# Final RMSNorm of a decoder trunk: sixteen tile buffers instead of six, and the loads in a loop of their own

## The chip, the cores and the metric

One core of a Trainium2 chip runs the whole program in one launch. The metric is the device time in microseconds, the median of several runs; lower is better. The profile is of one further execution.

## The reference, cut to what matters

The network has two residual layers over 2048 tokens of width 1024, each followed by a mixture of experts, and ends with one RMSNorm over every token. Only that last step is touched:

```python
def rmsnorm(x, gain):
    xf = x.astype(jnp.float32)
    y = xf * lax.rsqrt(jnp.mean(xf * xf, axis=-1, keepdims=True) + EPS)
    return (y * gain.astype(jnp.float32)).astype(x.dtype)
...
    return rmsnorm(x, final_norm)
```

So 2048 x 1024 float32 numbers (16 tiles of 128 rows, 512 KB each) are read, every row is scaled by its own factor and by the vector `final_norm`, and the same amount is written.

## The kernel before, in words

The trunk (`trunk`, L1661) runs layer 0, its experts, the DeltaNet mixer, its output projection, the second set of experts and then `final` (L1029). The experts scatter their rows into `acc`, a DRAM tensor, through indirect DMAs of GpSimd (L838), and end in a loop with a run-time count (`tc.For_i`, L985); every engine passes that point before `final` begins, so nothing of `final` runs beside the experts.

`final` opens the pool `fin`, loads the gain vector spread over 128 partitions into `fr` (L1033), and then has one loop over the NT = 16 tiles. Tile t is loaded from `acc` into `xin` (L1036; six buffers of 4 KB in each partition), ScalarE squares it and sums each row into `ss` (L1039), `rstd` turns the sum into a factor with a small VectorE instruction (L187) and a power on GpSimd (L189), VectorE multiplies the tile by the factor and by `fr` in place (L1041), and the tile is stored to the output (L1042). `ss1`, `rs1t` and `rs1` have four buffers each, from the pool `small` (L75).

All loads and stores of `final` are issued by SyncE (SP), on one queue, and SP issues in the order of its instruction list: a store that waits for VectorE holds up every load behind it. The list's order is made when the program is built. A scheduler takes the instructions that are ready in its own timing and, among those, the one written first. In the order that it made here SP has four loads, the four stores of the same tiles, four loads, and so on, although six buffers are there. The scheduler also gives the DMAs of this queue eight completion semaphores in turn, and a DMA waits until the one that had its semaphore before it has landed, so at most eight are in flight.

Of the kernel before, what the change touches and what calls it, by code (L numbers as in the profile page):

```python
# [6 lines left out]
F32 = mybir.dt.float32  # L7
# [9 lines left out]
P = 128  # L17
S = 2048
D = 1024
KD = D // P  # L20
EPS = 1e-6
NT = S // P
# [48 lines left out]
class Trunk:  # L71
# [957 lines left out]
    def final(self, out, l=1):  # L1029
        tc, nc = self.tc, self.nc  # L1030
        with tc.tile_pool(name="fin", bufs=3, reuse_waits="tile") as pool:
            fr = pool.tile([P, D], F32, name="fr", bufs=1)
            nc.sync.dma_start(fr, self.ins["final"].to_broadcast([P, D]))  # L1033
            for t in range(NT):
                x = pool.tile([P, D], F32, name="xin", bufs=6)
                nc.sync.dma_start(x, self.acc[t * P:(t + 1) * P])  # L1036
                ss = self.small.tile([P, 1], F32, name="ss1")
                sq = pool.tile([P, D], BF16, name="sqo", bufs=1)
                nc.scalar.activation(sq, x, AF.Square, accum_out=ss)  # L1039
                r = self.rstd(ss, 1.0 / D, 1, "rs1")  # L1040
                nc.vector.scalar_tensor_tensor(x, x, r, fr, op0=ALU.mult, op1=ALU.mult)  # L1041
                nc.sync.dma_start(out[t * P:(t + 1) * P], x)  # L1042
# [654 lines left out]
```

## Time and profile before

| what | us |
|---|---|
| median of 3 runs (lowest to highest) | 3322.71 (3316.65 to 3327.7) |
| the profiled execution, its own time | 3314.97 |
| span of its instructions | 3313.2 |
| first load of `final` issued | 3249.73 |
| `final` to the end of the span | 63.5 |

The profiled execution lies 7.74 us under the median of the runs, and its span 1.8 us under its own time. The times in the trace count from the start of the span. `final` is the last 1.9% of it. An engine or a DMA queue is read as busy, or as waiting for what ended its idle time. The DMA share is the mean busy share of the core's 16 DMA engines in a stretch; values a little over 1 come from overlapping records.

### The profile page before, as it was taken

What the parts mean: (1) busy time and instruction counts of PE and PEld (TensorE: products, weight loads), DVE (VectorE), ACT (ScalarE), POOL (GpSimd) and SP (SyncE); (2) the same over time, 40 slices, a digit from 0 to 9 for tenths busy, and PEclk for the clock granted to TensorE, in tenths of its full rate; (3) what the DMA queues carried; (4) which work ended last, traced back from release to release, by engine and by line L of the source; (5) the groups of instructions that cost most, each with busy time, mean ns of one, the idle gap of its engine ahead of it and who ended that gap; (6) DMA issues with size and microseconds to landing.
All of it is one profiled execution on the core that took longest, in us unless ns stands there. A gap on an engine that the chain in (4) does not pass through costs nothing. (4 is left out here: it accounts for less than half of the span.)

```text
span 3313.2 us, 41885 instructions
## 1 busy us (share of the span) xinstructions
PE 2908.4 (88%) x14192; PEld 2313.6 (70%) x14192; DVE 2443.9 (74%) x3805; ACT 1495.1 (45%) x2560; POOL 1022.7 (31%) x877
## 2 busy tenths in 40 slices
PE   4979878787999997999989999988988996999991
PEld 3756666566777774888867877777987765777770
DVE  4998999757878875777876786858445556888783
ACT  6135233216656546443444433444772214666552
POOL 0142323333443431322212131235530212434431
PEclk9989999898999998999999999998999997999996
DMA  6225233638999854545352343457957437989876
GB/s 222 85 73 209 83 132 127 216 121 303 309 281 298 268 169 160 171 153 191 136 174 83 104 144 106 144 148 223 268 195 227 153 121 253 308 279 297 264 232 217
DMA packets 384984, 633.37 MB, mean 191 GB/s; under 512 B 111232, under 2 KB 245504, under 8 KB 384768
## 3 DMA queue, kind: packets, MB, share of 16 engines
q1 hardware_dynamic: 355904, 563.38, 49.9%
q0 software_dynamic: 28864, 67.30, 8.7%
q8 instruction: 113, 1.85, 0.2%
q14 instruction: 103, 0.84, 0.1%
HBM read 484.46 MB, written 175.44 MB: 199 GB/s over the span
## 5 line engine op out<-in xcount | busy, mean ns | idle before, releaser
L260 PE MATMUL pm<-hh,wh 128*128 128x512 f32 x1408 | 565.9, 402 | 0.8 <-ACT wh L237 0.7
L262 PE MATMUL pm<-hh,wl 128*128 128x512 f32 x1408 | 556.5, 396 | 3.6 <-DVE wl L238 3.6
L261 PE MATMUL pm<-hl,wh 128*128 128x512 f32 x1408 | 555.4, 395 | 4.2 <-DVE hl L233 4.2
L238 DVE TENSOR_TENSOR wl<-wr,wh 128x1024 fp32r<-128x1024 f32 x384 | 452.2, 1218 | 40.7 <-ACT wh L237 37.3
L237 ACT ACTIVATE wh<-wr 128x1024 fp32r<-128x1024 f32 x384 | 399.5, 1057 | 134.7 <-PE py L851 56.8
L838 POOL DMA_INDIRECT acc<-ys,ixs x102 | 263.5, 2584 | 435.3 <-DVE wl L238 149.6
L261 PEld LDWEIGHTS pm<-hl,wh 128*128 128x128 f32 x1408 | 269.2, 191 | 63.4 <-DVE hl L233 4.6
L260 PEld LDWEIGHTS pm<-hh,wh 128*128 128x128 f32 x1408 | 269.1, 191 | 62.5 <-issue 4.6
L262 PEld LDWEIGHTS pm<-hh,wl 128*128 128x128 f32 x1408 | 268.6, 191 | 62.9 <-DVE wl L238 5.7
L817 PE MATMUL pu<-wh,xt 128*128 128x512 f32 x656 | 268.8, 410 | 0.5 <-ACT xt L237 0.5
L818 PE MATMUL pu<-wl,xt 128*128 128x512 f32 x656 | 261.3, 398 | 0.0
L819 PE MATMUL pu<-wh,xt 128*128 128x512 f32 x656 | 260.3, 397 | 0.0
L238 DVE TENSOR_TENSOR wl<-wraw,wh 128x1024 fp32r<-128x1024 f32 x88 | 110.9, 1261 | 155.4 <-ACT wh L237 155.2
L286 DVE SCALAR_TENSOR_TENSOR acc<-cin,wfir,acc 128x512 f32<-128x512 f32 (+1 forms) x320 | 214.7, 727 | 0.1
L536 PE MATMUL po<-woh,yh 128*128 128x512 f32 x512 | 172.4, 413 | 30.6 <-ACT yh L237 22.1
L237 ACT ACTIVATE wh<-wraw 128x1024 fp32r<-128x1024 f32 x88 | 93.2, 1059 | 227.4 <-PE pm L261 227.2
L1220 DVE SCALAR_TENSOR_TENSOR dacc<-ub,cols,dacc 128x1024 f32<-128x1024 f32 x144 | 186.8, 1297 | 2.8
L536 PE MATMUL po<-wol,yh 128*128 128x512 f32 x512 | 166.6, 405 | 0.0
L536 PE MATMUL po<-woh,yl 128*128 128x512 f32 x512 | 165.5, 402 | 0.3 <-DVE yl L238 0.3
L795 POOL DMA_INDIRECT xg<-hn,ixs x102 | 112.4, 1102 | 162.6 <-PE tp L805 87.3
L189 POOL TENSOR_TENSOR rs<-rs1t,expo 128x1 f32<-128x1 f32 x48 | 28.3, 589 | 381.1 <-DVE rs1t L187 339.6
L819 PEld LDWEIGHTS pu<-wh,xt 128*128 128x128 f32 x656 | 124.1, 189 | 30.8 <-DVE xt L238 0.5
(377 smaller groups left out, 6362.2 us busy)
## 6 DMA issues: line engine op xcount, KB each, us to landing
wr<-in_w_up_dram SPq DMA_DIRECT2D x256, 512.0 KB, 7.6
wr<-in_w_down_dram SPq DMA_DIRECT2D x128, 512.0 KB, 7.0
modw<-in_modwT_dram SPq DMA_DIRECT2D x96, 512.0 KB, 5.1
wraw<-in_w_in_dram SPq DMA_DIRECT2D x88, 512.0 KB, 3.6
stin<-stg SPq DMA_DIRECT2D x32, 1280.0 KB, 10.4
yr<-yT SPq DMA_DIRECT2D x32, 512.0 KB, 4.7
acc<-xo SPq DMA_DIRECT2D x32, 512.0 KB, 4.1
hn<-ho SPq DMA_DIRECT2D x32, 512.0 KB, 3.2
```

The costliest lines, as they stand in the source:

```text
L237: a = nc.scalar.activation(h, x, AF.Copy) if eng == "act" else nc.vector.tensor_copy(h, x)
L238: return a, nc.vector.tensor_sub(l, x, h.bitcast(F32))
L260: nc.tensor.matmul(ps, wh[:, k], hh[:, k], start=k == 0, stop=False)
L261: nc.tensor.matmul(ps, wh[:, k], hl[:, k], start=False, stop=False)
L262: nc.tensor.matmul(ps, wl[:, k], hh[:, k], start=False, stop=k == KD - 1)
L286: self.tap = nc.vector.scalar_tensor_tensor(o, x, w, i, op0=ALU.mult, op1=ALU.add)
L536: nc.tensor.matmul(ps[:, ns], a[:, k], b[:, ns], start=k == 0 and i == 0, stop=k == KD - 1 and i == 2)
L817: nc.tensor.matmul(ps, xh[:, k], uh, start=k == 0, stop=False)
L818: nc.tensor.matmul(ps, xh[:, k], ul, start=False, stop=False)
L819: nc.tensor.matmul(ps, xl[:, k], uh, start=False, stop=k == KD - 1)
L838: st = nc.gpsimd.indirect_dma_start(out=self.acc, out_offset=bass.IndirectOffsetOnAxis(ap=ix[:, 0:1], axis=0), in_=ys, in_offset=None, bou ...
L1220: nc.vector.scalar_tensor_tensor(acc, ub[:, i:i + 1024], self.col("dn_conv", si * 4 + i), acc, op0=ALU.mult, op1=ALU.add)
```

## The change

The loop is cut in two. The first loop allocates all sixteen tiles (`bufs=NT`, 64 KB in each partition instead of 24 KB) and issues all sixteen loads; the second does the arithmetic and the stores, as before. No instruction that computes or moves data is added or removed.

```diff
             fr = pool.tile([P, D], F32, name="fr", bufs=1)
             nc.sync.dma_start(fr, self.ins["final"].to_broadcast([P, D]))
+            xs = []
             for t in range(NT):
-                x = pool.tile([P, D], F32, name="xin", bufs=6)
+                x = pool.tile([P, D], F32, name="xin", bufs=NT)
                 nc.sync.dma_start(x, self.acc[t * P:(t + 1) * P])
+                xs.append(x)
+            for t, x in enumerate(xs):
                 ss = self.small.tile([P, 1], F32, name="ss1")
                 sq = pool.tile([P, D], BF16, name="sqo", bufs=1)
                 nc.scalar.activation(sq, x, AF.Square, accum_out=ss)
```

## Rows read from the trace of the kernel before

**Rows 1.** The chain that ended last, from 3240 us on: shares by line.
```profile
by line: DMA xin<-acc 24.8%; issue 18.7%; POOL rs L189 10.4%; DVE xin L1041 9.7%; DMA acc<-ys,ixs 6.6%; ACT sqo L1039 4.3%; DVE rs1t L187 3.0%; SPq L1036 1.3%; SPq L1042 1.2%; POOLq L1693 0.7%; SPq L985 0.5%; SPq L1033 0.4%; POOLq L944 0.3%
```

**Rows 2.** Timeline of SP's queue (start, us, what; one line merges several).
```profile
3249.73 0.34 SPq L1033 DMA_DIRECT2D fr<-in_final_dram  x1
3250.12 2.15 SPq L1036 DMA_DIRECT2D xin<-acc  x4
3258.86 6.35 SPq L1042 DMA_DIRECT2D out_dram<-xin  x4
3265.26 2.27 SPq L1036 DMA_DIRECT2D xin<-acc  x4
3273.81 6.54 SPq L1042 DMA_DIRECT2D out_dram<-xin  x4
...
3295.10 2.26 SPq L1036 DMA_DIRECT2D xin<-acc  x4
3303.01 6.54 SPq L1042 DMA_DIRECT2D out_dram<-xin  x4
```

**Rows 3.** Waits in `final`: total us, times, longest; ScalarE, then SP's queue.
```profile
ACT sqo L1039 <- DMA xin<-acc: 45.6, 5, 16.2
SPq L1042 <- DVE rs1t L187: 38.5, 12, 6.6
SPq L1042 <- DVE xin L1041: 6.5, 4, 1.7
```

**Rows 4.** Windows: stretch, us, PE, PEld, DVE, ACT, POOL busy, PEclk, DMA share, GB/s.
```profile
3249.73:3313.20 63.47, 0.00 (x0) 0.00 (x0) 21.94 (x32) 18.39 (x32) 8.68 (x16) 0.50 0.72 273
3254.00:3258.00 4.00, 0.00 (x0) 0.00 (x0) 0.60 (x2) 2.30 (x4) 0.57 (x1) 0.50 1.01 405
3260.90:3261.60 0.70, 0.00 (x0) 0.00 (x0) 0.05 (x2) 0.00 (x0) 0.54 (x1) 0.50 0.10 35
3265.30:3268.30 3.00, 0.00 (x0) 0.00 (x0) 0.00 (x0) 0.00 (x0) 0.00 (x0) 0.50 0.87 273
6.00:26.00 20.00, 4.99 (x16) 2.59 (x16) 9.07 (x23) 14.02 (x18) 1.02 (x1) 1.00 1.02 400
3304.00:3305.00 1.00, 0.00 (x0) 0.00 (x0) 1.00 (x2) 0.74 (x2) 0.00 (x0) 0.50 1.04 422
3311.82:3313.20 1.38, 0.00 (x0) 0.00 (x0) 0.00 (x0) 0.00 (x0) 0.00 (x0) 0.50 0.00 0
```

**Rows 5.** Timeline of the engines: first tile, then multiplies of the second group.
```profile
3255.53 1.06 ACT L1039 ACTIVATE sqo<-xin 128x1024 bf16<-128x1024 f32 x1 [16.18 <-DMA xin<-acc]
3257.55 1.29 DVE L1041 SCALAR_TENSOR_TENSOR xin<-xin,rs,fr 128x1024 f32<-128x1024 f32 x1 [0.69 <-POOL rs L189]
...
3276.63 1.28 DVE L1041 SCALAR_TENSOR_TENSOR xin<-xin,rs,fr 128x1024 f32<-128x1024 f32 x1 [0.72 <-POOL rs L189]
...
3278.70 1.29 DVE L1041 SCALAR_TENSOR_TENSOR xin<-xin,rs,fr 128x1024 f32<-128x1024 f32 x1 [0.72 <-POOL rs L189]
```

**Rows 6.** The instructions of `xin` from 3243 us on: ns min/median/max, starts.
```profile
L1036 SPq DMA_DIRECT2D xin<-acc x16: 376/431/783, 3250.1 to 3297.0; - x16
L1039 ACT ACTIVATE sqo<-xin x16: 1056/1056/1057, 3255.5 to 3303.6; 128x1024 bf16<-128x1024 f32 x16
L1041 DVE SCALAR_TENSOR_TENSOR xin<-xin,rs,fr x16: 1284/1285/1286, 3257.6 to 3307.9; 128x1024 f32<-128x1024 f32 x16
L1042 SPq DMA_DIRECT2D out_dram<-xin x16: 332/335/338, 3258.9 to 3309.2; - x16
```

**Rows 7.** Issue to landing of L1036's loads, then of L1042's stores.
```profile
DMA to landing us min/median/max: 4.4/6.0/7.5
...
DMA to landing us min/median/max: 2.6/2.6/3.0
```

**Rows 8.** Small instructions of `final` grouped by line (busy us, mean ns, idle before).
```profile
L189 POOL TENSOR_TENSOR rs<-rs1t,expo 128x1 f32<-128x1 f32 x16 | 8.7, 542 | 54.1 <-DVE rs1t L187 42.2 <-DMA xin<-acc 11.8
L1039 ACT ACTIVATION_READ_ACCUMULATOR sqo<-xin 128x1 f32 x16 | 3.0, 186 | 0.0
```

## The prediction, made before the changed kernel was run

> **What bounds the kernel now.** I read the chain that ended last first, because only the stretch that sets the end can pay. From 3240 us on, its largest share is the landing of the loads of `xin`, 24.8%, followed by the small steps between the engines ("issue", 18.7%) and GpSimd's power, 10.4% [rows 1]. So the end of the kernel is a chain of load, norm, load, norm, and no engine's work. The timeline of SP's queue says why: four loads, then four stores spread over 6.35 us, then four loads, in four cycles, the first 15.14 us from load to load (3250.12 to 3265.26), and so on to 3295.10 (the third of the four is left out of the rows) [rows 2]. The waits show both ends of this see-saw: ScalarE stands 45.6 us waiting for a load, and SP stands 38.5 + 6.5 = 45.0 us at stores whose tile VectorE has not finished, with the next four loads listed behind [rows 3]. The table by stretch shows what that costs the transfers. Over `final` the DMA engines are busy 0.72 of the time and move 273 GB/s. While four loads queue up they move 405 GB/s at a share of 1.01, between two stores 35 GB/s at 0.10 [rows 4]. So nothing is saturated as a whole, yet the DMA engines are saturated in each burst; the time lies between the bursts.
>
> A measure for the prize: 63.47 us at 273 GB/s are 17.3 MB, that is `fr`, sixteen loads and sixteen stores of 512 KB. At the 400 GB/s that the start of this kernel holds for 20 us [rows 4] they would take 43.3 us, leaving 20.2 us.
>
> **The change, part by part.**
>
> *Sixteen buffers.* Each partition holds 64 KB of `xin` instead of 24 KB. `final` comes behind the loop that all engines pass, so the memory is free by then; I cost this at nothing. The loads' waits for a store to free a slot go away; no load of the rows waited for one visibly, since the four stores stood in front of it anyway. Nothing to gain there by itself.
>
> *The loads move ahead of the stores on SP's queue.* The twelve loads of the later groups pass twelve stores in SP's list. Issue cost: a load takes 0.431 us of SP, the groups of four 2.15 to 2.27 us [rows 2, 6], so sixteen would take some 9 us, to about 3259. That is when the first store is ready now, 3258.86 [rows 2]. But at most eight DMAs of this queue are in flight, by the program's semaphores. Counted from `fr`, the ninth DMA is load 7 (the first is load 0): it waits for `fr` to land, and load 15 for load 7, which lands near 3255.5 + 7 x 1.31 = 3264.7; the first store then waits for load 8, near 3266.0. So the store is issued some 7 us later than now. This costs nothing as long as the DMA engines have loads to move meanwhile, and they have until 3275.2 (below). If that cover were gone, it would cost those 7 us once.
>
> *The sum.* The first load lands as now: ScalarE begins the first square at 3255.53, released by that load [rows 5]. One transfer at 400 GB/s takes 524,288 bytes / 400 GB/s = 1.31 us. Behind it come fifteen loads, 19.7 us, to 3275.2, and sixteen stores, 21.0 us, to 3296.1. From the last landing to the end of the span it is 1.38 us, with no DMA moving [rows 4]: 3297.5, against 3313.2 now, a change of -15.7 us. The other way round: of the 20.2 us that the transfers don't need, 3.2 us at the start (5.8 us from the issue of `fr` to the first square, less two transfers) and 1.4 us at the end stay, which leaves 15.6.
>
> *Does the arithmetic keep up?* ScalarE needs 1.056 + 0.186 = 1.24 us a tile, under the 1.31 us of a load [rows 6, 8]. The chain through VectorE and GpSimd is slower: one multiply begins 2.07 us after another (3276.63, 3278.70), because VectorE stands 0.72 us at GpSimd's power in every tile [rows 5]. The first multiply begins at 3257.55; sixteen end at 3257.55 + 15 x 2.07 + 1.29 = 3289.9, and a store lands 2.6 us after its issue [rows 7]: 3292.5. That is 3.6 us before the DMA engines are done, so this chain stays covered; it would take over if its pace rose above 2.31 us. The multiplies are 1284 to 1286 ns in all sixteen tiles, under every DMA load that occurs [rows 6], so I don't expect it to.
>
> *The unknown: a long run of stores.* No row shows one. Stores are now single bursts. From below: in a microsecond filled by one store 422 GB/s moved [rows 4], 1.24 us a transfer; with that for all 31 the end is 38.5 us behind 3255.5, at 3295.4 with the tail, a change of -17.8. From above: the slowest stretch in which SP never lacked something to issue is the turn from a store to loads, 273 GB/s at a share of 0.87 [rows 4], 1.92 us; sixteen such stores bring 3307.3, -5.9. I take 400 GB/s for both kinds, because that row is twenty microseconds of queued 512 KB transfers, which is what the queue will hold, and because a store's burst is as fast as a load's. A mean of up to 1.49 us over the 31 would still save 10 us.
>
> What is late next: the DMA engines themselves, first with loads, then with stores.
>
> The terms are against the profiled execution: 3314.97 - 15.7 = 3299.3. It lies 7.74 us under the median of the runs, 3322.71, from which I give the number: 3307.0.
>
> **The rivals.**
>
> *Stores back to back run slower than loads.* For it: the turn from a store to loads moved 273 GB/s at a share of 0.87 [rows 4], so each packet took longer there. Against it: single bursts at 422 and 405 GB/s. Halfway between 273 and 400, at 336 GB/s, a store takes 1.56 us, sixteen 25.0 us: 3301.6, a change of -11.6, 3311.1 on the median. The Trainium skill (DMA: Bandwidth & Descriptors, "Where 436 GB/s comes from") says that for transfers between HBM and SBUF the HBM side binds, at about 358 GB/s a core; by that, an estimate, all 31 transfers take 45.4 us, -10.9 us, 3311.8. This trace's 400 GB/s over 20 us contradicts it for loads; for stores no run here shows it yet.
>
> *The vector chain becomes the bound.* If sharing SBUF with an unbroken stream doubled the 0.72 us at the power, the pace would be 2.79 us, the last multiply would end at 3300.7 and the kernel at 3304.7: -8.5, 3314.2. Only the constant 1285 ns speak, and against it.
>
> *The order does not change.* If the scheduler still put stores between the loads in its list, the cycles of four would stay: 3322.7. For it: it did so with six buffers, so buffers alone never made the order. Against it: a load now is written ahead of every store and has its own buffer, so whenever SP is free a load comes first.
>
> *Slower: the stores run one at a time.* Now their waits fall into the time of arithmetic. If, when all sixteen come behind the loads, each waited for the landing of the one before, at the 3.0 us of the longest [rows 7], they would end at 3275.2 + 48.0 = 3323.2, the kernel at 3324.6: +11.4, 3334.1. It decides from 2.91 us a store on (at 2.6 us it is +5). Against it: four stores were issued within 6.35 us, one every 2 us [rows 2], with 2.6 us to land, so one did not wait for the other.
>
> **How the numbers follow.** A measurement of this kernel tells about 0.3% from no change, 10 us. Forecast 0.74, slow stores 0.13, vector chain 0.05, order unchanged 0.05, stores one at a time 0.03. The forecast is over 10 us in all but the far part of its bounds and the scatter of the runs (-6 to +5 us about their median): 0.70 of its 0.74. Slow stores lie near the line, 0.07 of 0.13; of the vector chain 0.04, since a smaller rise than the one priced is likelier. So faster 0.81, same 0.16, slower 0.03. The range goes from 3299 (the fast bound, 3304.9, less the scatter) to 3315, which takes in the slow stores with most of the scatter; above it lie the unchanged order, the slower rival and the far end of the stores' bound.
>
> **What would show it.** Right: in SP's timeline sixteen loads stand ahead of the first store; the table by stretch shows a share near 1 and about 400 GB/s from 3253 to 3296 without a hole; ScalarE's wait for loads falls from 45.6 us to less than 20, most of it before the first tile; SP's waits at stores shift from VectorE to the landing of earlier transfers; multiplies keep a pace of 2.07 us and are done some 6 us before the end. Wrong: a share well below 1 in the second half (the vector chain, or stores one at a time), a share of 1 with under 360 GB/s there (slow stores), or groups of four loads. Everything before 3249.73 should be the same; a difference there is the scatter of executions, not the change.

## The result, and the profile after

| kernel | median us (lowest to highest, runs) | ratio to the kernel before, 95% interval |
|---|---|---|
| before | 3319.68 (3310.48 to 3327.7, 8) | 1 |
| changed | 3298.89 (3292.06 to 3308.66, 8) | 0.9944, 0.9931 to 0.9957 |

The change is faster by 0.56%, which is 18.6 us of the median before (14.3 to 22.9 over the interval): small, but clear of the scatter. The two medians themselves lie 20.8 us apart. The profiled executions agree: the span is 3295.8 us instead of 3313.2, and the first load of `final`, that of `fr`, is issued at 3249.70 instead of 3249.73, so all 17.4 us lie in `final`: 46.1 us from the issue of `fr` to the end of the span instead of 63.5.

SP's queue in the changed kernel, from its timeline:

```profile
3249.70 0.34 SPq L1033 DMA_DIRECT2D fr<-in_final_dram  x1
3250.09 14.58 SPq L1037 DMA_DIRECT2D xin<-acc  x16
3265.68 24.05 SPq L1045 DMA_DIRECT2D out_dram<-xin  x16
```

The four cycles of [rows 2] are gone: sixteen loads, then sixteen stores. The first store goes out 6.8 us later than before (3265.68, before 3258.86). The table by stretch shows that nothing was lost by it (columns as in [rows 4]):

```profile
3249.70:3295.80 46.10, 0.00 (x0) 0.00 (x0) 21.68 (x32) 18.39 (x32) 8.67 (x16) 0.50 0.94 376
3249.70:3253.00 3.30, 0.00 (x0) 0.00 (x0) 0.00 (x0) 0.00 (x0) 0.00 (x0) 0.50 0.61 187
3254.00:3275.00 21.00, 0.00 (x0) 0.00 (x0) 12.30 (x19) 14.94 (x26) 4.89 (x9) 0.50 1.02 411
3275.00:3280.00 5.00, 0.00 (x0) 0.00 (x0) 2.88 (x5) 3.12 (x5) 1.62 (x3) 0.50 1.03 419
3285.00:3290.00 5.00, 0.00 (x0) 0.00 (x0) 2.94 (x5) 0.00 (x0) 1.08 (x2) 0.50 1.03 421
3290.00:3294.40 4.40, 0.00 (x0) 0.00 (x0) 0.00 (x0) 0.00 (x0) 0.00 (x0) 0.50 0.79 321
3294.40:3295.80 1.40, 0.00 (x0) 0.00 (x0) 0.00 (x0) 0.00 (x0) 0.00 (x0) 0.50 0.00 0
```

The share is 1.02 to 1.03 through loads and stores alike, against 0.72 over `final` before; it is lower in the first 3.3 us (0.61) and while the last stores run out (0.79), and nothing moves in the last 1.40 us (1.38 before). The work of VectorE, ScalarE and GpSimd is what it was (21.68, 18.39 and 8.67 us; 21.94, 18.39 and 8.68 before). What changed are the waits. ScalarE's wait for loads, and SP's own, in `final`:

```profile
ACT sqo L1042 <- DMA xin<-acc: 16.1, 2, 15.8
```

```profile
SPq L1037 <- DMA xin<-acc: 7.7, 8, 1.1
SPq L1045 <- DVE rs1t L187: 7.6, 5, 1.7
SPq L1045 <- DMA xin<-acc: 7.1, 8, 0.9
SPq L1696 <- DMA out_dram<-xin: 4.5, 1, 4.5
SPq L1045 <- DMA out_dram<-xin: 2.6, 3, 0.9
SPq L1045 <- DVE xin L1044: 2.0, 2, 1.7
```

ScalarE waits 16.1 us instead of 45.6, nearly all of it ahead of the first tile. In both totals the first wait (15.8 us here, 16.2 before) began some 10 us before `final`, while the experts still ran; inside `final` ScalarE waits about 6 us instead of about 35. SP waits 9.6 us at stores for VectorE instead of 45.0 [rows 3]. It now waits for the landing of earlier transfers (7.7 us at loads, 7.1 and 2.6 us at stores), which costs nothing, because the DMA engines stay busy with queued transfers (share 1.02 to 1.03). VectorE's multiplies and the time from issue to landing, loads then stores:

```profile
L1044 DVE SCALAR_TENSOR_TENSOR xin<-xin,rs,fr x16: 1283/1284/1286, 3257.2 to 3288.1; 128x1024 f32<-128x1024 f32 x16
...
DMA to landing us min/median/max: 5.1/10.2/10.4
...
DMA to landing us min/median/max: 5.0/9.8/10.2
```

The last multiply begins at 3288.1 and ends at 3289.4. Its store lands 5.0 us after its issue, at 3294.4, where a store alone takes 2.6 [rows 7]: it stands behind others. So the DMA queue should set the end, not the arithmetic. The chain that the profile follows back from the last instruction seems to say otherwise: from 3278.95 on it runs through VectorE and GpSimd to the last multiply at 3288.09, because that multiply released the last store. Such a chain doesn't say how much would be gained by shortening it; e6 and e7 below test that.

### The profile page after: what moved, and what is told of

The parts are those of the page before. It is cut to its first block, busy times and chain, and to the rows that moved or that the text cites. A ratio compares the mean times of both kernels' runs of the same rounds, so it can differ in the third digit from the quotient of the medians.

```text
span 3295.8 us, 41888 instructions
## 1 busy us (share of the span) xinstructions
PE 2909.2 (88%) x14192; PEld 2317.2 (70%) x14192; DVE 2442.8 (74%) x3805; ACT 1495.1 (45%) x2560; POOL 1029.7 (31%) x877
## 5 line engine op out<-in xcount | busy, mean ns | idle before, releaser
L819 PEld LDWEIGHTS pu<-wh,xt 128*128 128x128 f32 x656 | 124.3, 189 | 30.6 <-DVE xt L238 0.4
L817 PEld LDWEIGHTS pu<-wh,xt 128*128 128x128 f32 x656 | 124.6, 190 | 28.9 <-ACT xt L237 1.5
```

What stands on the lines that cost most here:

```text
L817: nc.tensor.matmul(ps, xh[:, k], uh, start=k == 0, stop=False)
L819: nc.tensor.matmul(ps, xl[:, k], uh, start=False, stop=k == KD - 1)
```

## The experiments

The measure is the stretch from the first DMA of `final` to the end of the span, in the profiled execution; it does not carry the scatter of the 3250 us ahead of it (the first DMA of `final` lay between 3247.5 and 3253.9 in all runs but one). Ratios are to the kernel before.

| kernel | `final`, us | ratio, 95% interval |
|---|---|---|
| before | 63.5 | 1 |
| changed | 46.1 | 0.9944, 0.9931 to 0.9957 |
| e1 sixteen buffers alone | 63.0 | 1.0007, 0.9996 to 1.0018 |
| e2 loads five ahead, six buffers | 55.4 | 0.9979, 0.9966 to 0.9992 |
| e3 stores on ScalarE's queue, six buffers | 48.9 | 0.9966, 0.9953 to 0.9979 |
| e4 gain vector early | 44.7 | 0.9964, 0.9954 to 0.9973 |
| e5 loads eight ahead, sixteen buffers | 46.1 | one run, no ratio |
| e6 without the power | 45.8 | one run, no ratio |
| e7 half of the stores | 43.7 | one run, no ratio |
| e8 loads five ahead, sixteen buffers | 47.5 | one run, no ratio |
| e9 changed, again | 46.1 | 0.9953, 0.9937 to 0.9969 |
| e10 loads eight ahead, again | 46.0 | 0.9948, 0.9933 to 0.9964 |
| e11 gain vector early, again | 45.5 | 0.994, 0.9925 to 0.9956 |

**e1: the buffers alone.**

```diff
-                x = pool.tile([P, D], F32, name="xin", bufs=6)
+                x = pool.tile([P, D], F32, name="xin", bufs=NT)
```

> The kernel before with sixteen buffers for xin and nothing else; load and store of a tile still stand in one loop, and SP's list still has four loads, four stores, four loads. Theory A (the order of loads and stores on SP's queue made the gain, the buffers only allow it): from the issue of fr to the end of the span it takes 63.5 us as before, within 0.5, and SP still waits some 45 us at stores for VectorE. Rival (a load waited for a buffer, so the buffers alone do it): 46 us, as in the changed kernel, and some 17 us less in all.

```profile
3251.89 0.34 SPq L1033 DMA_DIRECT2D fr<-in_final_dram  x1
3252.28 2.63 SPq L1036 DMA_DIRECT2D xin<-acc  x4
3260.86 6.35 SPq L1042 DMA_DIRECT2D out_dram<-xin  x4
3267.26 2.25 SPq L1036 DMA_DIRECT2D xin<-acc  x4
```

```profile
SPq L1042 <- DVE rs1t L187: 37.1, 12, 6.1
SPq L1042 <- DVE xin L1041: 6.6, 4, 1.7
```

SP's timeline has the cycles of [rows 2], and SP waits 37.1 + 6.6 us at stores. `final` takes 63.0 us and the ratio is 1.0007. Buffers that nobody issues into are worth nothing; theory A holds.

**e2: the order alone, with six buffers.**

```diff
+            xs = []
+            def fetch(t):
+                if t < NT:
+                    x = pool.tile([P, D], F32, name="xin", bufs=6)
+                    nc.sync.dma_start(x, self.acc[t * P:(t + 1) * P])
+                    xs.append(x)
+            for t in range(5):
+                fetch(t)
             for t in range(NT):
-                x = pool.tile([P, D], F32, name="xin", bufs=6)
-                nc.sync.dma_start(x, self.acc[t * P:(t + 1) * P])
+                fetch(t + 5)
+                x = xs[t]
```

> Only the order, with the six buffers of before: each tile's load is written five tiles ahead of its arithmetic. SP's list then has six loads, and after that three stores and three loads in turn. Theory A (all that counts is that the DMA engines, or VectorE's chain, never run dry): the next three loads are issued behind the third store, near 3263, and land about 5 us later, before VectorE needs them, so the chain of 2.07 us a tile runs without a hole to about 3289.4, and fr to the end of the span takes 46 to 48 us. Rival B (a turn between stores and loads on the queue costs about 1 us, as the stretch of 273 GB/s behind a store suggests): four turns, 50 us. Rival C (sixteen buffers are needed): 55 us or more.

SP's queue in e2, from its timeline, and SP's waits:

```profile
3251.92 3.77 SPq L1039 DMA_DIRECT2D xin<-acc  x6
3260.49 4.35 SPq L1052 DMA_DIRECT2D out_dram<-xin  x3
3264.93 2.85 SPq L1039 DMA_DIRECT2D xin<-acc  x3
3267.87 3.12 SPq L1052 DMA_DIRECT2D out_dram<-xin  x3
3274.28 2.81 SPq L1039 DMA_DIRECT2D xin<-acc  x3
```

```profile
SPq L1039 <- DMA out_dram<-xin: 18.3, 9, 5.1
SPq L1052 <- DVE rs1t L187: 10.5, 6, 4.8
SPq L1052 <- DVE xin L1051: 7.4, 2, 5.8
```

Theory A fell here: 55.4 us, less than half of the gain. I had reckoned the first turn about right (loads behind the third store, 3264.93; `fr` goes out 1.8 us later here than in the changed kernel) and stopped there. A load waits until the store that used its buffer has landed, 18.3 us in nine waits, all but 1.7 us of it from the second turn on, where that store has been queued behind three loads. So SP stands still, and VectorE runs dry. With six buffers the order alone is not enough.

**e3: no new order, no new buffer, but the stores on another queue.**

```diff
-                nc.sync.dma_start(out[t * P:(t + 1) * P], x)
+                nc.scalar.dma_start(out[t * P:(t + 1) * P], x)
```

> The kernel before, with its one loop and six buffers; only the stores are issued by ScalarE on its own queue, so no store stands in front of a load on SP's. ScalarE's list is square of tile t+1, store of tile t. Theory A (what cost the time before was loads held up behind stores that wait for VectorE): a load now waits for its buffer alone, fr to the end takes 46 to 49 us, and SP no longer waits for VectorE. Rival (one queue must have its loads together, or mixed loads and stores slow each other): 52 us or more. A store that waits in ScalarE's list could also hold up the squares: then VectorE would wait for ScalarE, and its pace would rise over 2.07 us a tile.

SP's waits and the table by stretch (all of `final`, then without its ends):

```profile
SPq L1036 <- DMA out_dram<-xin: 29.4, 10, 9.8
```

```profile
3253.47:3302.40 48.93, 0.00 (x0) 0.00 (x0) 22.28 (x32) 18.40 (x32) 8.70 (x16) 0.50 0.92 354
3261.47:3298.40 36.93, 0.00 (x0) 0.00 (x0) 21.94 (x31) 16.36 (x30) 8.13 (x15) 0.50 1.00 390
```

48.9 us: 14.5 of the 17.4 us from one word, with the old loop. SP no longer waits for VectorE at all, only for buffers (29.4 us). That shows the cause directly: loads were held up by stores that waited for VectorE on the same queue. A second queue is not faster in itself: 390 GB/s without the ends, under the 411 to 421 of the one filled queue of the changed kernel. 2.8 us more than with all loads ahead remain. Most of them can be found in the table by stretch:

```profile
3268.00:3273.00 5.00, 0.00 (x0) 0.00 (x0) 3.43 (x6) 2.50 (x6) 1.08 (x2) 0.50 1.00 279
```

Here SP issues its loads singly, as buffers come free, and the share is 1.00 at only 279 GB/s, so a full share alone doesn't show a full rate. From 3266 to 3273 the mean is 292 GB/s; against the 419 of the stretch behind it that is about 2.1 us (an estimate). ScalarE also waits 6.3 us behind its own stores; what that costs was not separated.

**e4: the gain vector loaded during the experts.**

```diff
+            if l:
+                self.fr = raw.tile([P, D], F32, name="fr", tag="wr")
+                nc.sync.dma_start(self.fr, ins["final"].to_broadcast([P, D]))
             with tc.For_i(0, more, 1):
...
-            fr = pool.tile([P, D], F32, name="fr", bufs=1)
-            nc.sync.dma_start(fr, self.ins["final"].to_broadcast([P, D]))
+            fr = self.fr
...
-        T.final(out)
+            T.final(out)
```

> The changed kernel, with the gain vector fr loaded during the experts into one of the eight buffers of their weights, so that the first load of final is that of tile 0. Theory A (the DMA engines set the end of final, with 33 transfers in a row): one transfer less, so the stretch from the first DMA of final to the end of the span falls from 46.1 us by the 1.24 to 1.3 us of a transfer and the 0.4 us of its issue, to 44.5. Rival (VectorE's chain or a fixed latency sets it): the chain also starts earlier, but the first load's landing keeps its 5 us from issue, so only 0.4 us goes. The experts have a buffer less at their end: they may lose some us before final, which is read apart. In all about 1.5 us under the changed kernel, too little for the timed ratio to show.

```profile
3211.84 0.34 SPq L987 DMA_DIRECT2D fr<-in_final_dram  x1
3253.85 5.16 SPq L1040 DMA_DIRECT2D xin<-acc  x10
```

```profile
3253.85:3298.50 44.65, 0.00 (x0) 0.00 (x0) 21.68 (x32) 18.39 (x32) 8.70 (x16) 0.50 0.94 376
```

`final` loses 1.45 us, a transfer and its issue, as theory A has it. The timed ratio came out above that of the changed kernel; e11 times it again.

**e5: loads eight tiles ahead, sixteen buffers.** The edit is that of e2 with `range(8)`, `fetch(t + 8)` and `bufs=NT`.

> The changed kernel with its loads written eight tiles ahead instead of all sixteen: SP's list has nine loads, then a store and a load in turn seven times, then nine stores. The DMA engines have the same 33 transfers. Theory A (only holes count): the queue holds enough at all times, fr to the end of the span takes 46 us, within 1. Rival B (each turn from a store to a load costs about 1 us, after the 273 GB/s that the kernel before showed there): seven turns, 52 to 53 us, with a DMA share near 1 but under 380 GB/s where they mix.

SP's timeline at the start of the mixed part, and the table by stretch:

```profile
3247.93 5.74 SPq L1039 DMA_DIRECT2D xin<-acc  x9
3256.69 0.34 SPq L1052 DMA_DIRECT2D out_dram<-xin  x1
3257.07 0.43 SPq L1039 DMA_DIRECT2D xin<-acc  x1
```

```profile
3247.54:3293.60 46.06, 0.00 (x0) 0.00 (x0) 21.66 (x32) 18.39 (x32) 8.68 (x16) 0.50 0.95 376
3263.00:3274.00 11.00, 0.00 (x0) 0.00 (x0) 6.94 (x11) 5.58 (x11) 3.13 (x6) 0.50 1.03 420
```

Loads and stores in turn move 420 GB/s. Rival B is out: the 273 GB/s behind the stores before [rows 4] were not a price of the turn. They belong to loads that start into an almost empty queue: e4, where the first loads have neither `fr` nor a store in front of them, shows the same share at a still lower rate, and 418 GB/s a microsecond later.

```profile
3254.80:3256.30 1.50, 0.00 (x0) 0.00 (x0) 0.00 (x0) 0.00 (x0) 0.00 (x0) 0.50 0.87 218
```

Why packets take longer there no run shows.

**e6 and e7: which of the two sets the end.** e6 uses the sum of squares as the factor:

```diff
-                r = self.rstd(ss, 1.0 / D, 1, "rs1")
+                r = ss
```

> The changed kernel without the small VectorE instruction and GpSimd's power: the multiply takes the sum of squares itself as its factor. It leaves out the mean, the epsilon and the reciprocal root. Theory A (the DMA engines set the end of final): VectorE's pace falls from 2.07 to about 1.3 us a tile, the stores are ready earlier, and the end does not move: 46.1 us within 0.5. Rival (VectorE's chain sets it): sixteen tiles save 15 x 0.77 = 11.5 us of the chain, and final falls until something else binds, by several us.

e7 stores every second tile:

```diff
-                nc.sync.dma_start(out[t * P:(t + 1) * P], x)
+                if t % 2:
+                    nc.sync.dma_start(out[t * P:(t + 1) * P], x)
```

> The changed kernel with the stores of the even tiles left out: half of the output is not written. Theory A (the DMA engines bind, VectorE's chain is 2.4 us behind them): the engines would be done after the loads and eight stores, at about 3284.5, so the end passes to the chain, whose last multiply ends at 3289.4 and whose store lands 2.6 us later: fr to the end 43.7 us, 2.4 less than the changed kernel, and the last store takes 2.6 us to land instead of 5.0. Rival one (the chain bound already): 46.1, no change. Rival two (the DMA engines alone matter): 36 us.

The table by stretch and VectorE's timeline of e6:

```profile
3250.42:3296.20 45.78, 0.00 (x0) 0.00 (x0) 20.33 (x16) 18.39 (x32) 0.00 (x0) 0.50 0.96 378
```

```profile
3260.03 14.10 DVE L1044 SCALAR_TENSOR_TENSOR xin<-xin,ss,fr 128x1024 f32<-128x1024 f32 x11
3274.42 3.67 DVE L1044 SCALAR_TENSOR_TENSOR xin<-xin,ss,fr 128x1024 f32<-128x1024 f32 x3 [0.29 <-ACT sqo L1042]
```

The same of e7, and the landing of its stores:

```profile
3249.82:3293.50 43.68, 0.00 (x0) 0.00 (x0) 21.66 (x32) 18.39 (x32) 8.68 (x16) 0.50 0.77 300
```

```profile
3288.23 1.29 DVE L1044 SCALAR_TENSOR_TENSOR xin<-xin,rs,fr 128x1024 f32<-128x1024 f32 x1 [0.72 <-POOL rs L189]
```

```profile
DMA to landing us min/median/max: 2.6/5.1/10.1
```

In e6 VectorE is done at 3278.1, 27.7 us behind the issue of `fr` instead of 39.7, and the end stays (45.8 us instead of 46.1). In e7 the DMA engines have eight transfers less, some 10 us, and the end moves by only 2.4 us, to the last multiply (3289.5) plus the 2.6 us of a store that stands alone. Both came as theory A said: the DMA engines set the end, and VectorE's chain lies 2.4 us behind them.

**e8: the order of e2 with sixteen buffers.** The edit is that of e2 with `bufs=NT`.

> The kernel with loads written five tiles ahead, with sixteen buffers instead of six. SP's list has six loads, then a store and a load in turn, and no load waits for a buffer. Theory D (with six buffers the loads lost their time waiting for the store before them in their buffer to land, and those stores lay behind queued loads): the 18.3 us of such waits are gone and fr to the end of the span takes 46 us, within 1, as with all loads ahead, against 55.4 with six buffers. Rival (five tiles are too few to keep the queue filled, or the turns between stores and loads cost): 50 us or more. SP should wait for VectorE at each early store, some 1.5 us, at no cost.

```profile
SPq L1052 <- DVE rs1t L187: 19.6, 13, 5.7
SPq L1052 <- DVE xin L1051: 6.3, 3, 2.7
```

```profile
3252.00:3257.00 5.00, 0.00 (x0) 0.00 (x0) 1.29 (x2) 2.87 (x5) 0.57 (x1) 0.50 1.02 415
3257.00:3262.00 5.00, 0.00 (x0) 0.00 (x0) 3.03 (x7) 4.03 (x8) 1.62 (x3) 0.50 0.94 370
3277.00:3282.00 5.00, 0.00 (x0) 0.00 (x0) 3.43 (x5) 2.01 (x5) 1.08 (x2) 0.50 1.02 419
```

47.5 us against 55.4: no load waits for a buffer (SP's waits above are at stores, for VectorE), and the mixed part runs at 419 GB/s. So the buffers were what e2 lacked, though its list also alternates one by one where e2's goes by threes. It misses the expected 46 within 1 by 0.5; the table shows a thin stretch at the first stores, 370 GB/s at 0.94. Five tiles ahead leave the queue short there: loads stand again behind stores that wait for VectorE, 19.6 + 6.3 us in all, and this is not quite free.

**e9, e10 and e11: three kernels timed side by side.** They are the changed kernel, e5 and e4 without an edit.

> The changed kernel as it is, timed beside the two that follow. Theory A: fr to the end of the span takes 46.1 us again, and the time is 0.993 to 0.996 of the kernel before. It is the yardstick: what differs between the three before final begins is scatter of executions if it does not come back in the ratios.

> Loads eight tiles ahead, sixteen buffers, timed. Theory A: final takes 46.06 us as in the look at it and the ratio to the kernel before is that of the changed kernel, within 0.15%. Rival B (turns between loads and stores cost about 1 us each): 7 us, 0.2%, slower than the changed kernel.

> The gain vector loaded during the experts, timed again beside the changed kernel. Theory A: final takes 44.65 us, 1.45 less, so the ratio is 0.0004 below that of the changed kernel, which the interval cannot tell from none. Rival (the buffer that fr takes, or its load, slows the part before final): the ratio stays some 0.002 above that of the changed kernel, as in the first timing, and the first DMA of final is issued some 4 us later than in the changed kernel.

The changed kernel's ratio is 0.9953 here, loads eight ahead 0.9948, the gain vector early 0.994: the intervals overlap by most of their width. In e11 `final` took 45.5 us, 0.8 more than e4 and than expected, and why is open; its first load was issued at 3261.44, later than in any other run; in e4 it was issued at 3253.85. In both the lag behind the changed kernel stood already when the second experts loaded their first weights (2764.87 in e4 and 2772.24 in e11, 2760.49 in the changed kernel: 4.4 and 11.8 us) and did not grow up to `final`, and the ratio did not stay above, so the rival of e11 is not borne out. The scatter of the part before `final` goes with TensorE's granted clock: of the eight runs of the changed kernel the shortest, 3292.06 us, had a mean of 0.948 of full speed and the longest, 3308.66, one of 0.943. No run shows that the clock is its cause. A version that beats the changed kernel by a measurable amount was not found; in the profile, loading the gain vector early saves 0.6 to 1.5 us.

## Why the prediction was right

*The bound.* The reading of the chain and the waits held: [rows 3] named the two halves of one fault, ScalarE at loads and SP at stores, and e3 shows that these were one fault, since moving the stores off SP's queue removed SP's wait for VectorE and 14.5 us without touching the loop or the buffers. One figure of it was too large: of ScalarE's 45.6 us some 10 lie before `final`.

*The order of issue.* Sixteen loads ahead of the first store, as said; load 15 and the first store went out at 3264.4 and 3265.68 (said: 3264.7 and 3266.0). The delay of 7 us for the first store was free, since the share stayed at 1.02. One sign came only in part: SP's waits at stores shifted to the landing of earlier transfers by half (9.7 us), and 9.6 us stayed with VectorE.

*The sum.* -15.7 us was said, -17.4 came in the profile and -18.6 in the ratio, whose interval holds both. The mechanism is right and one term was mis-sized: 1.31 us a transfer, from 400 GB/s. Loads moved at 411 GB/s, 524,288 bytes in 1.28 us, and stores at 419 to 421, 1.25 us. Fifteen and sixteen of them make 39.2 us instead of 40.6, which is 1.4 of the 1.7 us; the other 0.3 us is the first load, which ScalarE took up at 3255.2. The low end of the bounds, 422 GB/s and -17.8, was nearer than the value I took, and it was a row of a store's burst, the very thing that was asked for. The other bound rested on a wrong reading: 273 GB/s was not the slowest stretch in which SP had something to issue. From 3250 to 3253 in the same trace, with four loads being issued, it was 188 at a share of 0.72; both are starts into an almost empty queue and say nothing of a long run of stores. The measured median, 3298.89, stands at the lower edge of the range, 0.1 us under 3299. Of the 8.1 us between it and 3307.0, 1.7 us are the sum and 3.0 us the kernel before, whose median over eight runs is 3319.68 instead of 3322.71; the other 3.4 us are the difference between the medians (20.8 us apart) and the two profiled executions (17.4), which nothing here traces further. Where the median falls against the range is largely chance: timed again (e9), the same kernel has a median of 3304.52, well inside.

*The arithmetic.* 3289.9 was said for the last multiply's end, 3289.4 came. e6 and e7 confirm that it is covered, by 2.4 us (3.6 said, as the transfers were taken too slow).

*The rivals.* Slow stores: refuted, 421 GB/s. The Trainium skill's 358 GB/s for HBM and SBUF (DMA: Bandwidth & Descriptors, "Where 436 GB/s comes from") does not hold in this run for loads or stores. The Trainium skill (HBM Reference, "Specifications (TRN2)") also says that a core streaming alone measures about 425 GB/s; with 411 to 421 on the only core in use the trace agrees with that figure. The vector chain: its multiplies kept 1284 ns under a full stream. Unchanged order: refuted by the timeline. Stores one at a time: refuted, each landed 9.8 us after its issue in the median, with one done every 1.25 us, so about eight were in flight.

*The one thing reasoned too lightly.* The prediction put the sixteen buffers at nothing by themselves, and e1 bears that out (1.0007). But it also let it seem that order alone does the work, and e2 shows that with six buffers the same kind of order brings 8.1 of 17.4 us. On one queue the gain is a product: the order fills the queue, and the buffers let it stay full.

## What to carry to other kernels

Where one queue issues loads and stores, look at what its instructions wait for: a store that waits for arithmetic holds up every load listed behind it, and more buffers don't help until the list is changed or the stores go to another queue. Issuing loads further ahead needs buffers for all of them, since a buffer is only free when its store has landed, and a store behind queued loads lands late. Price the result by the longest saturated stretch that the trace has, and prefer a row of the same kind of transfer.

## What the runs showed of the hardware

A stretch of low rate behind a store (273 GB/s at a share of 0.87) looked like a cost of turning from writing to reading. It was the start into an almost empty queue, and loads with nothing in front of them show it too (218 GB/s at 0.87 in e4). With the queue kept filled, loads and stores in turn moved 420 GB/s (e5), and sixteen stores in a row 419 to 421. So a busy share near 1 is not yet a full rate: it stood beside 279 GB/s where loads came singly (e3) and beside 420 where many were queued (e5). The time from issue to landing is mostly place in the queue: 2.6 us for a store that stands alone, 9.8 us in the median with about eight in flight, at no cost in rate.
